# Index scores summed straight from PSUM, with the u projection moved behind them, in a hybrid decoder layer

## The chip, the cores and the metric

The kernel runs on one core of a Trainium2 chip. The metric is device time in microseconds (us) of one execution. TensorE is PE in the profile, ScalarE is ACT, VectorE is DVE, GpSimd is POOL, SyncE is SP, which issues the DMAs. SBUF is the on-chip memory; PSUM takes the results of matmuls, in 8 banks of 512 fp32 columns on each of 128 partitions.

## The reference, cut to what matters

One decoder layer over 1024 tokens of width 1024. A projection of the normalised input gives u (512 columns, for a state-space head group "S5"), q, k and v (attention) and q_idx, k_idx, w_idx (8 index heads of 64). The index heads choose 256 keys for each query; attention (a softmax over those keys alone) and the complex state-space recurrence of S5 follow, then an output projection and a squared-ReLU MLP.

```python
def block(start):                       # 128 queries
    causal = key_pos[None, :] <= q_pos[:, None]
    logits = jax.nn.relu(jnp.einsum('bthd,bsd->bths', qib, k_idx_f))
    score = jnp.einsum('bth,bths->bts', wb, logits) * IDX_SCALE
    score = jnp.where(causal[None], score, -jnp.inf)
    _, sel = lax.top_k(score, topk)     # topk = 256
    ...

h = rms_norm(x, norm1_g[i]) * (1.0 + sc1) + sh1
u_ssm, q, k, v, q_idx, k_idx, w_idx = jnp.split(h @ w_in[i], split_points, axis=-1)
y_ssm = s5_mixer(u_ssm, lam_re[i], lam_im[i], log_dt[i], ssm_b_re[i], ssm_b_im[i],
                 ssm_c_re[i], ssm_c_im[i], d_skip[i], w_glu[i], b_glu[i])
y_att = dsa_attention(q, k, v, q_idx, k_idx, w_idx, q_gain[i], k_gain[i])
mixed = jnp.concatenate([rms_norm(y_ssm, gn_ssm[i]), rms_norm(y_att, gn_attn[i])], axis=-1)
x = x + g1 * (mixed @ w_out[i])
...
```

## The kernel before, in words

Every matmul of the projections is made of three (`mm3`, L90 to L92): the operands are split into a high part (`wh`, `hh`) and a low part (`wl`, `hl`) in fp32r. `load_w` fetches a weight in pieces `raw` (two buffers); ACT makes `wh`, POOL makes `wl` (six buffers each; a half of u or q needs four of each). The product has 128 tokens and 256 columns.

The stage of the change:

- `index_proj` works through c = 0 to 3, two index heads at a time. `index_q` projects the index queries of c + 1; `index_score` makes the scores of c for the query tiles qt = 2 to 7 (the first two tiles need no selection): TensorE multiplies against the high and the low part of the index keys (L551, L552) into two PSUM banks (`bank2`, tag S, two such pairs; `bank`, tag g, gives four single banks), ACT takes Relu times |w| into an SBUF tile `r` (L556), and DVE adds sign(w) times r to the score tile `sc` in SBUF (L558 for the first head, L560). At the end six DVE operations (L517) put the causal mask on the last 128 columns of each tile.
- `tab` is a generator of tables for the state-space part, eight of them (b = 0 to 7): GpSimd operations (`cx`, `cl`, `mx`, `mt`, `tx`, `pt`) and stores to memory. It is woven into `index_proj`, one step at a time, and then into the projections.
- `proj_qu` projects u in two halves (each tile of 128 tokens copied by ACT to `us`, L576, and stored by SP) and then q in two halves (copied by ACT, L590; squared by POOL).
- `select` finds a threshold a tile so that 256 scores pass it: `bn_stats` of the tiles, a first guess v and its step gs, then nine rounds of counting, three tiles on DVE (L711, L721) and three on ACT (Sign with a running sum, L707, L717), a last step on DVE with the eight largest values (L734 to L741), and a flag: `bad` is summed over the partitions by a small matmul, copied, and read by the engines, which skip a slower search if it is 0. `need` is how many of the tied scores to keep. Then each tile's mask is made: Sign on ACT (L785), a scan and three passes on DVE, a product on POOL (L790).
- Attention and the state-space part follow; attention's first matmuls transpose q (L1222), ACT copies them (`qT`, L1224).

The kernel is written as Python generators, interleaved by `weave`; a scheduler of the framework then puts the instructions of each engine in one fixed order when the program is built, by the priority at which each was written. Each engine, and SP's queue of DMA issues, works through its order from the front, and an instruction that waits holds those behind it. `issue_after` names an instruction after which the framework places others.

## Time and profile before

| | |
|---|---|
| median of 3 runs | 1361.43 us (1357.9 to 1364.48) |
| the profiled execution | 1360.31 us, its span 1358.5 us |
| busy share of the span | PE 90%, DVE 75%, ACT 45%, POOL 27% |
| granted clock of TensorE, mean | 0.942 of 2.4 GHz |
| index scores end | 241.9 us after the span's start |
| first copy of attention | 319.33 us |

A row of the trace names the line, the engine, the operation, the tile written and the tiles read, the shape, and then busy time and mean or start and duration. "[8.99 <-DMA raw<-w_in]" means that the engine stood idle for 8.99 us before it and that this DMA was what it waited for. PEclk is the share of full clock granted to TensorE.

### The profile page before, as it was taken

How to read it: one execution, taken by the hardware profiler on the slowest of the kernel's cores; microseconds unless marked ns; L12 is line 12 of the kernel's file. 1: busy time of each engine (PE TensorE's matmuls, PEld its weight loads, DVE VectorE, ACT ScalarE, POOL GpSimd, SP SyncE). 2: the span in 40 equal slices, each digit the busy share in tenths (PEclk: the TensorE clock that was granted, in tenths of full speed). 3: DMA queues.
4: the chain of work that ended last, by engine and by line, in shares of the span. 5: the costliest groups of instructions: out<-in, count | busy, mean ns of one | idle time of the engine just before them, and what ended most of it. 6: DMA issues, size and time to landing. Idle time of an engine off the chain costs nothing.

```text
span 1358.5 us, 18554 instructions
## 1 busy us (share of the span) xinstructions
PE 1216.1 (90%) x6414; PEld 1038.1 (76%) x6414; DVE 1017.4 (75%) x1894; ACT 616.7 (45%) x1231; POOL 364.7 (27%) x350
## 2 busy tenths in 40 slices
PE   4987987935898999999979999999988999999997
PEld 4876887934788889888857788888866878788785
DVE  6599947897978763347795677677678888876887
ACT  6454453584777775724242333333224334333330
POOL 3072799861643453711100000000000000000125
PEclk9797989975899997999989999999998999999999
DMA  9511122350231572422412444433457735436252
GB/s 330 131 41 40 60 97 91 133 149 9 71 103 51 179 231 71 133 78 93 160 66 93 148 146 163 155 141 138 163 197 275 254 95 193 132 95 210 84 185 109
DMA packets 119327, 179.83 MB, mean 132 GB/s; under 512 B 28864, under 2 KB 63680, under 8 KB 119232
## 3 DMA queue, kind: packets, MB, share of 16 engines
q1 hardware_dynamic: 118160, 178.61, 40.1%
q8 instruction: 50, 0.82, 0.3%
q14 instruction: 45, 0.37, 0.1%
q10 hardware_dynamic: 1072, 0.03, 0.0%
HBM read 128.92 MB, written 48.50 MB: 131 GB/s over the span
## 4 chain that ended last, share of the span: by engine, by line
PE 51%; DVE 12%; DMA 4%; ACT 2%; issue 2%; POOL 2%; SPq 1%; DVEq 0%; ACTq 0%; POOLq 0%
PE pS L90 10%; PE pS L91 10%; PE pS L92 10%; PE pg L90 5%; PE pg L91 5%; PE pg L92 5%; DMA awa<-w_ada 2%; PE po L1274 2%; DVE fm L472 2%; PE pg L269 1%; PE pg L1258 1%; DVE acc L1871 1%; DVE acc L1845 1%; DVE fw L472 1%; POOL wol L472 1%
## 5 line engine op out<-in xcount | busy, mean ns | idle before, releaser
L1845 POOL TENSOR_TENSOR acc<-acc,g 128x512 f32<-128x512 f32 x4 | 5.9, 1499 | 579.1 <-DVE acc L1871 579.1
L91 PE MATMUL pg<-wl,hh 128*128 128x256 f32 (+1 forms) x288 | 81.6, 284 | 13.0 <-POOL wl L472 13.0
L470 ACT ACTIVATE fm<-ar 128x512 fp32r<-128x512 f32 x56 | 34.9, 624 | 119.9 <-PE pg L91 55.1
L90 PE MATMUL pg<-wh,hh 128*128 128x256 f32 (+1 forms) x288 | 81.0, 285 | 3.7 <-ACT wh L470 2.6
L1274 PEld LDWEIGHTS po<-v,pt 128*128 128x128 f32 x576 | 77.5, 208 | 6.0 <-ACT pt L1261 3.8
L1274 PE MATMUL po<-v,pt 128*128 128x64 f32 x576 | 78.8, 285 | 3.5 <-ACT pt L1261 3.3
L92 PE MATMUL pg<-wh,hl 128*128 128x256 f32 (+1 forms) x288 | 81.4, 284 | 0.0
L560 DVE SCALAR_TENSOR_TENSOR sc<-r,wsgn,sc 128x384 f32<-128x384 f32 (+5 forms) x42 | 56.0, 1344 | 28.5 <-ACT r L556 27.3
L90 PE MATMUL pS<-fm 128*128 128x512 f32 x160 | 62.2, 400 | 4.7 <-DVE z L1874 4.4
L91 PEld LDWEIGHTS pg<-wl,hh 128*128 128x128 f32 x288 | 55.1, 191 | 14.0 <-POOL wl L472 13.4
L91 PE MATMUL pS<-fm 128*128 128x512 f32 x160 | 63.1, 397 | 0.3 <-DVE fm L472 0.3
L92 PE MATMUL pS<-fm 128*128 128x512 f32 x160 | 62.9, 395 | 0.0
L1245 DVE CUSTOM_DVE_ANT_0 P<-pS,sc,rq 128x384 f32<-128x384 f32 (+5 forms) x48 | 43.9, 941 | 20.9 <-PE pS L1241 12.8
L90 PEld LDWEIGHTS pg<-wh,hh 128*128 128x128 f32 x288 | 54.3, 190 | 5.0 <-ACT wh L470 2.8
L556 ACT ACTIVATE r<-pS,wabs 128x384 f32<-128x384 f32 (+5 forms) x48 | 40.6, 848 | 36.4 <-PE pS L552 27.7
L92 PEld LDWEIGHTS pg<-wh,hl 128*128 128x128 f32 x288 | 54.9, 191 | 0.4
L470 ACT ACTIVATE fw<-ax 128x512 fp32r<-128x512 f32 x42 | 26.2, 623 | 61.1 <-PE pS L91 29.6
L1261 ACT ACTIVATE pt<-pg 128x512 f32<-128x512 f32 (+1 forms) x80 | 42.2, 547 | 22.2 <-PE pg L1258 21.8
L1258 PE MATMUL pg<-ident,P 128*128 128x128 f32 x288 | 49.2, 292 | 3.0 <-DVE zl L1340 1.3
L1247 ACT ACTIVATE P<-P,mx 128x128 f32<-128x128 f32 (+7 forms) x64 | 49.1, 769 | 5.7 <-DVE mx L1245 5.5
L90 PE MATMUL pS<-woh,mh 128*128 128x512 f32 x128 | 51.2, 400 | 0.0
L92 PE MATMUL pS<-woh,ml 128*128 128x512 f32 x128 | 50.9, 398 | 0.0
(606 smaller groups left out, 4154.1 us busy)
## 6 DMA issues: line engine op xcount, KB each, us to landing
awa<-w_ada SPq DMA_DIRECT2D x32, 512.0 KB, 4.3
a_d<-ws SPq DMA_DIRECT2D x64, 256.0 KB, 2.7
wr<-w_ff SPq DMA_DIRECT2D x32, 512.0 KB, 6.3
w1r<-w_ff SPq DMA_DIRECT2D x15, 1024.0 KB, 5.2
ax<-a_d SPq DMA_DIRECT2D x56, 256.0 KB, 2.8
ar<-a_d SPq DMA_DIRECT2D x56, 256.0 KB, 2.9
a_d<-c SPq DMA_DIRECT2D x45, 256.0 KB, 2.0
x<-x SPq DMA_DIRECT2D x16, 512.0 KB, 5.1
```

The lines of the kernel that those rows point to most:

```text
L90: T.matmul(out, lh, rh, start=start, stop=False, **kw)
L91: T.matmul(out, lh, rl, start=False, stop=False, **kw)
L92: self.pe = T.matmul(out, ll, rh, start=False, stop=stop, **kw).ins
L470: nc.scalar.activation(hi, x, AF.Copy)
L472: e.tensor_tensor(lo, x, f(hi), op=OP.subtract)
L556: S.activation(rv, ps[:, :, :n], AF.Relu, scale=self.wabs[:, qt, h:h + 1])
L560: V.scalar_tensor_tensor(sc, rv, self.wsgn[:, qt, h:h + 1], sc, op0=OP.mult, op1=OP.add)
L1245: V.tensor_tensor_reduce(pv, ps[:, :nj, :m], bv, scale=self.rq[:, qt, h:h + 1], scalar=-NEG, op0=OP.add, op1=OP.min, accum_out=mx)
L1247: S.activation(p[:, :w], p[:, :w], AF.Exp, scale=-1.0, bias=mx, accum_out=LS[qt][:, h:h + 1])
L1258: T.transpose(ps[:, o:o + 128], P[n][h][:, (k0 + i) * 128:(k0 + i + 1) * 128], self.ident)
L1261: S.activation(pt[:, :m], ps[:, :m], AF.Copy)
L1274: T.matmul(po[:, o:o + HD], pt[:, (2 * i + h) * 128:(2 * i + h + 1) * 128], self.v[:, k0 + i, kv * HD:(kv + 1) * HD], start=(o == 0 and k0 ...
```

## The change

1. `index_score` works on one bank at a time: tiles of up to 512 keys take a single bank from tag g, the others a pair whose halves are handled apart. Relu is written in place in PSUM; DVE reads it there and adds into `sc`. The tile `r` is gone. For h = 0 the last 128 columns get the mask as an addend (0 or NEG) in the same operation, and the six mask operations at the end go. ACT has 80 Relus in place of 48, DVE 86 operations in place of 54.
2. The matmuls of u are placed behind the last score matmul (`issue_after`).
3. Only four tables are woven into `index_proj`. From b = 4 on each begins with a small GpSimd copy from `self.gate`, which is `gs` for b = 4, 5, 6 and `need` for b = 7, and no table step is taken in the projections before the gate is set.
4. The rounds of `select` update t and v one column at a time.
5. The flag's matmul and copy become a DMA of `bad` (128 floats) into one row and a DVE maximum.

```diff
-LATER, TABN = 500, 1
+LATER, TABN, TABG = 500, 1, 4
...
-            self.index_proj(ix, tab)
+            self.gate = None
+            self.index_proj(ix, itertools.islice(tab, 10 * TABG))
...
-                next(tab, None)
+                if self.gate is not None and i < 29:
+                    next(tab, None)
...
-        nc.vector.tensor_scalar(self.caus, io, 0.0, 0.5, op0=OP.is_le, op1=OP.subtract)
-        nc.vector.tensor_scalar(self.caus, self.caus, -NEG, 2.0, op0=OP.mult, op1=OP.mult)
+        nc.vector.tensor_scalar(self.caus, io, 0.0, NEG, op0=OP.is_gt, op1=OP.mult)
...
-        for qt in range(2, 8):
-            dg = self.bias[qt][:, qt * 128:]
-            V.scalar_tensor_tensor(dg, dg, NEG, self.caus, op0=OP.max, op1=OP.min)
...
         nc = self.nc
         V, S, G, T = nc.vector, nc.scalar, nc.gpsimd, nc.tensor
         for qt in range(2, 8):
-            n = (qt + 1) * 64
+            w = (qt + 1) * 128
+            nj = 1 if w <= 512 else 2
+            n = w // nj
             for i in range(2):
                 h = 2 * c + i
-                ps = self.bank2()
+                ps = self.bank()[:, None, :] if nj == 1 else self.bank2()
                 lq = qs[c][i][:, (qt - 2) * 128:(qt - 1) * 128]
-                for j in range(2):
+                for j in range(nj):
                     o = ps[:, j, :n]
-                    T.matmul(o, lq, self.kih[:, j * n:(j + 1) * n], start=True, stop=False)
-                    T.matmul(o, lq, self.kil[:, j * n:(j + 1) * n], start=False, stop=True)
-                sc = self.bias[qt].rearrange("p (j n) -> p j n", j=2)
-                r = ix.tile([128, L], F32, name="r", tag="r", bufs=3)
-                rv = r[:, :2 * n].rearrange("p (j n) -> p j n", j=2)
-                S.activation(rv, ps[:, :, :n], AF.Relu, scale=self.wabs[:, qt, h:h + 1])
-                if h == 0:
-                    V.tensor_scalar(sc, rv, self.wsgn[:, qt, h:h + 1], None, op0=OP.mult)
-                else:
-                    V.scalar_tensor_tensor(sc, rv, self.wsgn[:, qt, h:h + 1], sc, op0=OP.mult, op1=OP.add)
+                    ks = slice(j * n, (j + 1) * n)
+                    T.matmul(o, lq, self.kih[:, ks], start=True, stop=False)
+                    self.last_sc = T.matmul(o, lq, self.kil[:, ks], start=False, stop=True).ins
+                    S.activation(o, o, AF.Relu, scale=self.wabs[:, qt, h:h + 1])
+                    sc, sg = self.bias[qt][:, ks], self.wsgn[:, qt, h:h + 1]
+                    if h:
+                        V.scalar_tensor_tensor(sc, o, sg, sc, op0=OP.mult, op1=OP.add)
+                        continue
+                    d = n - 128 if j == nj - 1 else n
+                    V.tensor_scalar(sc[:, :d], o[:, :d], sg, None, op0=OP.mult)
+                    if d < n:
+                        V.scalar_tensor_tensor(sc[:, d:], o[:, d:], sg, self.caus, op0=OP.mult, op1=OP.add)
                 yield
 
     def proj_qu(self):
...
-                for k in range(KC):
-                    wh, wl = wg[k]
-                    self.mm3(ps[:, :256], self.hh[:, k, tl], self.hl[:, k, tl], wh, wl, k == 0, k == KC - 1)
+                with self.tc.issue_after(self.last_sc):
+                    for k in range(KC):
+                        wh, wl = wg[k]
+                        self.mm3(ps[:, :256], self.hh[:, k, tl], self.hl[:, k, tl], wh, wl, k == 0, k == KC - 1)
...
+        self.gate = gs
...
-        ps = self.bank()
-        T.matmul(ps[0:1, 0:1], bad, self.ones[:, 0:1], start=True, stop=True)
+        row = sp.tile([1, 128], F32, name="row")
+        nc.sync.dma_start(row, bad)
-        V.tensor_copy(fi, ps[0:1, 0:1])
+        V.tensor_reduce(fi, row, axis=AX.X, op=OP.max)
...
+        self.gate = need
...
+            if b >= TABG:
+                G.tensor_copy(cx[:, 0, 0:6], self.gate)
```

TensorE before, in the scores of c = 1: score matmuls (pS) and, between them, matmuls of the u projection (pg, with wh and wl of w_in).

```order
L92 MATMUL pg_2199<-wh_2183,hl_125 128x256
L90 MATMUL pg_2199<-wh_2189,hh_124 128x256
L551 MATMUL pS_1708<-kih_135,qs_1427 128x256
L552 MATMUL pS_1708<-kil_136,qs_1427 128x256
L551 MATMUL pS_1708<-kih_135,qs_1427 128x256
L552 MATMUL pS_1708<-kil_136,qs_1427 128x256
L91 MATMUL pg_2199<-wl_2190,hh_124 128x256
```

TensorE after the change, in the scores of c = 2 and 3 (single banks are named pg here too), and where the scores end:

```order
L553 MATMUL pS_1906<-kih_134,qs_1652 128x320
L554 MATMUL pS_1906<-kil_135,qs_1652 128x320
L553 MATMUL pg_2023<-kih_134,qs_1843 128x384
L554 MATMUL pg_2023<-kil_135,qs_1843 128x384
L553 MATMUL pS_1922<-kih_134,qs_1653 128x320
L554 MATMUL pS_1922<-kil_135,qs_1653 128x320
L553 MATMUL pg_2029<-kih_134,qs_1844 128x384
L554 MATMUL pg_2029<-kil_135,qs_1844 128x384
L553 MATMUL pg_2034<-kih_134,qs_1843 128x512
```

```order
L553 MATMUL pS_2107<-kih_134,qs_1844 128x512
L554 MATMUL pS_2107<-kil_135,qs_1844 128x512
L91 MATMUL pg_2156<-wh_2134,hh_123 128x256
L92 MATMUL pg_2156<-wl_2135,hh_123 128x256
L93 MATMUL pg_2156<-wh_2134,hl_124 128x256
```

No u matmul stands between scores any more; the first (wh, hh) comes right behind the last score matmul.

POOL before, where u's second half has its last two low parts (wl_2538, wl_2544); cx, cl, mt, tx and pt belong to tables:

```order
L1025 TENSOR_TENSOR cx_1931<-A2_619,Li_949 128x576 [waits Pool_49]
L472 TENSOR_TENSOR wl_2538<-raw_2535,wh_2537 128x512 [waits Activation_49]
L472 TENSOR_TENSOR wl_2544<-raw_2541,wh_2543 128x512 [waits DMAHW7_49,Activation_49]
L1056 TENSOR_TENSOR pt_1863<-e1c_950,e2c_952 128x256 [waits DMAHW4_49]
L1056 TENSOR_TENSOR pt_1863<-e1c_950,e2s_953 128x256
L1027 TENSOR_TENSOR cl_1930<-A1_618,Lr_948 128x576 [waits DMAHW5_49]
L1059 TENSOR_TENSOR pt_1863<-pt_1863,tx_1864 128x256 [waits Pool_49] x2
```

POOL after the change, where u's second half has its last two low parts (wl_2496, wl_2502); gs is the selection's, and the tables are 4 and 5. First the gate, then the weights:

```order
L1053 TENSOR_TENSOR mt_1958<-mt_1958,mx_1959 128x512 [waits Pool_49]
L1066 TENSOR_TENSOR pt_2000<-pt_2000,tx_2001 128x256 [waits Pool_49] x2
L1034 TENSOR_TENSOR cl_2350<-A1_617,Lr_947 128x576 [waits DMAHW1_49,Pool_49]
L1051 TENSOR_TENSOR mt_2459<-D1_555,Lr_947 128x512 [waits DMAHW2_49,Pool_49]
L1029 COPY cx_2351<-gs_2314 128x6 [waits DVE_49]
L1049 TENSOR_TENSOR mx_2460<-D2_556,Li_948 128x512
```

```order
L1063 TENSOR_TENSOR pt_3034<-e1c_949,e2c_951 128x256 [waits DMAHW3_49]
L1063 TENSOR_TENSOR pt_3034<-e1c_949,e2s_952 128x256
L1053 TENSOR_TENSOR mt_2905<-mt_2905,mx_2906 128x512 [waits Pool_49]
L1066 TENSOR_TENSOR pt_3034<-pt_3034,tx_3035 128x256 [waits Pool_49]
L474 TENSOR_TENSOR wl_2496<-raw_2493,wh_2495 128x512 [waits Activation_49]
L1066 TENSOR_TENSOR pt_3034<-pt_3034,tx_3035 128x256 [waits Pool_49]
L474 TENSOR_TENSOR wl_2502<-raw_2499,wh_2501 128x512 [waits Activation_49]
```

Before, the low parts of u's second half stood between operations of tables that wait for no gate; now the gate of tables 4 and 5 stands ahead of them.

ACT after the change, in the last of the selection's rounds (ja with c is a count, t and v its update); wh_ are high parts of q's first half, us tiles of u:

```order
L580 ACTIVATE us_2716<-pg_2691 128x256 [waits DMAHW1_49,PE_49]
L724 ACTIVATE v_2308<-t_2310,v_2308,st2_2317 128x1 [waits Activation_49]
L723 ACTIVATE t_2310<-c_2309,oA_1260 128x1 [waits Activation_49]
L722 ACTIVATE ja_2213,c_2309<-sc4_103,v_2308 128x640
L724 ACTIVATE v_2308<-t_2310,v_2308,st2_2317 128x1 [waits Activation_49]
L723 ACTIVATE t_2310<-c_2309,oA_1260 128x1 [waits Activation_49]
L722 ACTIVATE ja_2213,c_2309<-sc6_105,v_2308 128x896
L580 ACTIVATE us_2763<-pg_2738 128x256 [waits DMAHW3_49,PE_49]
L724 ACTIVATE v_2308<-t_2310,v_2308,st2_2317 128x1 [waits Activation_49]
L472 ACTIVATE wh_2833<-raw_2831 128x512 [waits DMAHW5_49,PE_49,Pool_49]
```

The high parts stand between counts of the selection, and each waits for TensorE (PE) to give a buffer back.

## Rows read from the trace of the kernel before

**Rows 1.** The page, busy us (share of span) xinstructions of each engine.

```profile
PE 1216.1 (90%) x6414; PEld 1038.1 (76%) x6414; DVE 1017.4 (75%) x1894; ACT 616.7 (45%) x1231; POOL 364.7 (27%) x350
```

**Rows 2.** Windows: stretch, us, busy (instructions) PE, PEld, DVE, ACT, POOL, PEclk, DMA share, GB/s.

```profile
160.00:200.00 40.00, 34.11 (x250) 33.20 (x250) 23.62 (x21) 19.35 (x31) 40.00 (x34) 0.91 0.23 78
200.00:240.00 40.00, 32.88 (x241) 31.65 (x240) 28.18 (x20) 17.87 (x27) 40.00 (x31) 0.91 0.31 102
280.00:300.00 20.00, 5.91 (x51) 5.71 (x49) 19.88 (x68) 19.97 (x60) 13.91 (x23) 0.75 0.58 160
300.00:320.00 20.00, 1.99 (x11) 1.99 (x12) 18.50 (x78) 0.69 (x2) 0.65 (x4) 0.50 0.24 71
320.00:340.00 20.00, 16.19 (x97) 14.62 (x96) 13.53 (x49) 14.18 (x45) 5.33 (x8) 0.64 0.04 8
340.00:360.00 20.00, 16.79 (x134) 15.27 (x132) 19.06 (x45) 17.80 (x41) 13.16 (x11) 1.00 0.22 53
```

**Rows 3.** Timeline of ACT and DVE: start us, us, instruction, idle before and releaser.

```profile
197.67 0.63 ACT L470 ACTIVATE wh<-raw 128x512 fp32r<-128x512 f32 x1 [8.99 <-DMA raw<-w_in]
...
240.39 1.51 DVE L560 SCALAR_TENSOR_TENSOR sc<-r,wsgn,sc 128x1024 f32<-128x1024 f32 x1 [9.59 <-ACT r L556]
```

**Rows 4.** The page, costliest groups: count, busy us, mean ns, idle before, releaser.

```profile
L91 PE MATMUL pg<-wl,hh 128*128 128x256 f32 (+1 forms) x288 | 81.6, 284 | 13.0 <-POOL wl L472 13.0
...
L560 DVE SCALAR_TENSOR_TENSOR sc<-r,wsgn,sc 128x384 f32<-128x384 f32 (+5 forms) x42 | 56.0, 1344 | 28.5 <-ACT r L556 27.3
```

**Rows 5.** Groups by shape, 113 to 243 us, DVE and ACT, columns as in rows 4.

```profile
L517 DVE SCALAR_TENSOR_TENSOR sc<-sc,caus 128x128 f32<-128x128 f32 x6 | 5.0, 827 | 0.2
L538 DVE TENSOR_TENSOR qs<-pg,qs 64x512 fp32r<-64x512 f32 x7 | 4.8, 686 | 0.1
L538 DVE TENSOR_TENSOR qs<-pg,qs 64x256 fp32r<-64x256 f32 x8 | 3.4, 422 | 0.3
...
L558 DVE TENSOR_SCALAR sc<-r,wsgn 128x1024 f32<-128x1024 f32 x1 | 0.7, 749 | 0.0
...
L556 ACT ACTIVATE r<-pS,wabs 128x1024 f32<-128x1024 f32 x8 | 8.9, 1115 | 4.4 <-PE pS L552 4.4
...
L556 ACT ACTIVATE r<-pS,wabs 128x384 f32<-128x384 f32 x8 | 4.6, 581 | 4.3 <-PE pS L552 4.2
```

**Rows 6.** Lines 576 and 590, the copies of u and q: durations min/median/max ns, first and last start.

```profile
L576 ACT ACTIVATE us<-pg x16: 369/383/388, 153.9 to 226.9; 128x256 f32<-128x256 f32 x16
...
L590 ACT ACTIVATE q<-pg x16: 361/383/391, 242.8 to 286.1; 128x256 f32<-128x256 f32 x16
```

**Rows 7.** Timeline of PE in the q projection, two matmuls with 24 between them.

```profile
279.77 0.28 PE L90 MATMUL pg<-wh,hh 128*128 128x256 f32 x1
...
282.70 0.28 PE L91 MATMUL pg<-wl,hh 128*128 128x256 f32 x1
```

**Rows 8.** Timeline of ACT: the selection's first and last round, attention's first copy, first mask.

```profile
257.37 1.04 ACT L707 ACTIVATE ja<-sc,v 128x896 bf16<-128x896 f32 x1 [6.57 <-DVE v L698]
...
299.70 0.39 ACT L719 ACTIVATE v<-t,v,st 128x1 f32<-128x1 f32 x1
...
319.33 0.60 ACT L1224 ACTIVATE qT<-pg 128x512 fp32r<-128x512 f32 x1 [19.24 <-PE pg L1222]
322.71 0.61 ACT L785 ACTIVATE ja<-sc,ntau 128x384 bf16<-128x384 f32 x1 [2.79 <-DVE ntau L779]
```

**Rows 9.** Line 1029, one operation of each of the eight tables, columns as in rows 6.

```profile
L1029 POOL TENSOR_TENSOR cl<-cl,cx x8: 1398/1792/2275, 155.4 to 273.5; 128x576 f32<-128x576 f32 x8
```

**Rows 10.** Groups of lines 787 to 789 on DVE, 320 to 372 us, columns as in rows 4.

```profile
L787 DVE TENSOR_TENSOR_SCAN pre<-eq 128x384 f16<-128x384 bf16 (+5 forms) x6 | 9.7, 1615 | 0.1
...
L788 DVE TENSOR_SCALAR eq<-pre,need 128x384 bf16<-128x384 f16 (+5 forms) x6 | 3.3, 552 | 0.0
L789 DVE TENSOR_TENSOR eq<-eq,ja 128x384 bf16<-128x384 bf16 (+5 forms) x6 | 3.2, 538 | 0.0
```

**Rows 11.** DMA issues: queue, operation, count, KB each, median us from issue to landing.

```profile
dg<-d_skip SPq DMA_DIRECT2D x8, 4.0 KB, 2.6
```

**Rows 12.** Windows, one stretch ahead of the scores, columns as in rows 2.

```profile
92.00:96.00 4.00, 2.42 (x12) 1.69 (x11) 3.86 (x10) 1.42 (x9) 2.02 (x3) 1.00 0.52 132
```

More of the change, by code (lines that the diff above doesn't have):

```diff
@@ L1 @@
+import itertools
 from contextlib import ExitStack
@@ L440, in k_norm @@
         self.rstd(rk, self.kss[:, 4 * hf:4 * hf + 4].rearrange("p t h -> p (t h)"), HD, ix)
-        knd = ix.tile([128, NKV, 4, 2, HD], F32, name="knd", tag="r", bufs=3)
+        knd = ix.tile([128, NKV, 4, 2, HD], F32, name="knd", bufs=2)
         yield
@@ L694, in select @@
         V.tensor_tensor(sd, va, y, op=OP.mult)
-        v, d, c, t = st(6, "v"), st(NV, "d"), st(6, "c"), st(6, "t")
+        v, c, t = st(6, "v"), st(6, "c"), st(6, "t")
         V.tensor_tensor(v, sd, self.zrow, op=OP.mult)
@@ L711, in select @@
             V.tensor_scalar(jv[:, :W[i]], B[i], col(v, i), None, op0=OP.is_ge, op1=OP.add, accum_out=col(c, i))
-        V.scalar_tensor_tensor(t[:, :NV], c[:, :NV], TOPK - 0.5, gs[:, :NV], op0=OP.subtract, op1=OP.mult)
-        V.tensor_tensor(v[:, :NV], v[:, :NV], t[:, :NV], op=OP.add)
+            V.tensor_scalar(col(t, i), col(c, i), TOPK - 0.5, col(gs, i), op0=OP.subtract, op1=OP.mult)
+            V.tensor_scalar(col(v, i), col(v, i), col(t, i), None, op0=OP.add)
         yield
@@ L721, in select @@
                 V.tensor_scalar(jv[:, :W[i]], B[i], col(v, i), None, op0=OP.is_ge, op1=OP.add, accum_out=col(c, i))
-            V.tensor_tensor(d, v[:, :NV], st1[:, k, :NV], op=OP.subtract)
-            V.scalar_tensor_tensor(t[:, :NV], c[:, :NV], float(TOPK), st2[:, k, :NV], op0=OP.is_ge, op1=OP.mult)
-            V.tensor_tensor(v[:, :NV], d, t[:, :NV], op=OP.add)
+                V.tensor_scalar(col(t, i), col(c, i), float(TOPK), st2[:, k, i:i + 1], op0=OP.is_ge, op1=OP.mult)
+                V.tensor_scalar(col(v, i), col(v, i), st1[:, k, i:i + 1], col(t, i), op0=OP.subtract, op1=OP.add)
             yield
```

## The prediction

> **What bounds the kernel now.** I read the busy shares first [rows 1]. TensorE leads with 90%, yet a share over the whole span says nothing about one stage, so I went to the stretches of the stage that the change touches [rows 2]. From 160 to 240 us TensorE is busy for 34.1 and 32.9 of each 40 us while DVE has only 23.6 and 28.2, and GpSimd is full. There TensorE does index scores and the u projection in turn, and both wait for GpSimd: ACT stands idle for 8.99 us until a raw piece of w_in lands, DVE for 9.59 us before its very last score [rows 3]; over the kernel TensorE loses 13.0 us to wl<-raw on GpSimd [rows 4]. The last score ends at 240.39 + 1.51 = 241.9 us [rows 3]. Then the picture turns over: from 280 to 320 TensorE works 5.9 and 2.0 us of 20 and its clock is at 0.50, half of 2.4 GHz, while DVE is full. The q projection is over (its last copy starts at 286.1 [rows 6]) and attention cannot start, because the flag's matmul stands ahead of it in TensorE's order: ACT takes the first qT only at 319.33, after 19.24 us of idling, and the first mask at 322.71 [rows 8]. So the stage is a chain: scores until 241.9, selection until about 318, attention after it, with TensorE empty for some 30 us.
>
> **Scores, c = 1 to 3.** The adds that read r and sc from SBUF average 1344 ns [rows 4]. They now read PSUM and one SBUF tile. The nearest rows are the subtractions qs<-pg, one PSUM and one SBUF input, made in the same stretch beside the same full GpSimd: 422 ns for 256 columns, 686 for 512 [rows 5], that is 0.16 us + 1.03 ns a column. A head's ten pieces (384, 512, and twice 320, 384, 448 and 512) cost 5.9 us against 6 x 1.344 = 8.1; six heads save 12.7 us. DVE's 23.6 + 28.2 = 51.8 us after 160 [rows 2] become 39.1. ACT gets four more Relus a head: 1115 and 581 ns for 1024 and 384 columns [rows 5] leave 0.26 us fixed, so six heads add 6.3 us; the u copies that leave (16 x 0.383 [rows 6]) take about as much out; ACT stays near 37 us. TensorE, rid of u, is no longer the bound: 16,896 columns a c at 0.457 ns (25 matmuls of 256 columns in 2.93 us [rows 7]) are 7.7 us. With GpSimd's weights out of the way the last score then ends at 160 + 39 = 199 us; a pair of PSUM banks is now held until DVE has read it, so I take **200** (194 to 212).
>
> **c = 0 and the mask: nothing.** The h = 0 products read PSUM instead of SBUF. From SBUF 1024 columns took 749 ns [rows 5], so 4,224 columns cost 3.1 us at least; by the PSUM price above they cost 5.9, with six more pieces 1.0 on top. The Trainium skill, VectorE: DVE Perf Modes, section "Why PSUM operands drop a tier", speaks against the change here: a PSUM operand holds an fp32 operation to one element a cycle. By the SBUF price this part would gain 3 us, by that rule it costs about what I have. Against the 3.8 us lost stand the six mask operations, 5.0 us [rows 5], which are gone.
>
> **Projections.** Held behind the last score matmul, u and q now run in one piece. Sixteen q copies from 242.8 to 286.1 [rows 6] are 2.89 us each, 23.1 a half; four halves 92.4 us from 199 on. The cost is the price of what hid u before: all 46 us of it lay under the scores. Then the gate. GpSimd waits for gs. The way from the last add to the first Sign takes 257.4 - 241.9 = 15.5 us now [rows 3, 8]; as the other tiles' statistics are placed among the last scores I take 8 (4 to 15). Behind gs stand tables 4 and 5 and behind these the weights wl of u's second half. Eight tables take 155.4 to 273.5, 16.9 us apiece with a wl in each [rows 9]; at the fastest row's pace, 1398 against a median of 1792, some 13. Two, less what stands ahead of the gate, are 21 to 28 us, so wl comes at 231 to 238, while TensorE wants it at 199 + 23.1 + 1.4 = 223.5: a hole of 7 to 14, I take **11** (none if gs is early and DVE quiet, 25 if gs is late). Projections end at 199 + 92 + 11 = **302**.
>
> **Selection.** From first Sign to last v 299.7 - 257.4 = 42.3 us, then 23.0 to the first mask [rows 8]. ACT's order now has the wh pieces of q between the Signs, and these wait until TensorE frees a buffer at the end of u's second half, about 200 + 55; the last round follows, so the first mask stands at about 200 + 81 = 281. The masks' scans, compares and products take DVE 9.7 + 3.3 + 3.2 us [rows 10]; all lies before 302. So the DMA in the flag's place costs nothing: at 2.6 us for a small load (dg<-d_skip [rows 11]; a matmul and a copy before) the projections hide it, and were selection last it would cost 2 to 4 us. The per-column operations lie beside ACT's longer chain: nothing. The gate on need holds the last table to about 276, and SP's loads for the state-space part stand behind its three stores, but attention comes first: nothing, or the store's few us if they are late.
>
> **What follows.** Attention starts at 302 instead of 318.7 (the first qT's wait ended): 17 us. Its first 40 us were slow: TensorE had 16.2 of 20 at a clock of 0.64, then 16.8 of 20 [rows 2]. A TensorE that never stopped enters at full clock: 16.2 x 0.36 = 5.8 us at most; the masks no longer share DVE, which is full at 340 to 360: at most the 7 us that TensorE idles. I take 8 of these (0 to 13). **Sum: 25 us.** Against the profiled 1360.3 that is 1335; the median of the runs is 1.1 higher, so **1336**.
>
> **The rivals.**
> - *Bank turns (slower).* Relu in place holds each pair of banks through TensorE, ACT and DVE: 4 x 0.23, then 2 x 0.69, then 0.69 for the last half [rows 5, 7], 3.0 us, of which half is gained if the two pairs overlap fully. If only one is ever in flight, eight pairs are 24 us a c and 26 with the singles: scores end at 160 + 78 = 238, projections at 340, and 21 - 8 = 13 us are lost: **1374**. It decides from a last score at 225 on, where nothing is left. For it: u no longer fills TensorE's waits. Against: ACT sits between and both halves have their own operations. 0.15.
> - *The gate starves TensorE (same).* The 13.0 us of wl [rows 4] show how easily GpSimd's order holds TensorE. A hole of 25 instead of 11, and 5 more at q's weights, end the projections at 321; the warm clock is all that is left: gain 0 to 8, **1357**. 0.17.
> - *A cold clock in the scores.* TensorE had 2.42 of 4 us busy at clock 1.00 once [rows 12] and 2.0 of 20 at 0.50 [rows 2]; the scores would give it 7.7 of 13. At half clock a c is 15.4 us, more than DVE's 11.9: 10.5 us later, **1347**. The Trainium skill, TensorE: Matmul & The Clock Gate, section "A second HAM failure mode: psum-queue depth-cycling", describes this: short idling between groups that turn through PSUM lets the clock fall again and again. Rows at a like share are all at 1.00. 0.08.
> - *More is freed.* No hole, the last score at 194, and all 13 us of the attention's start: 38 to 45 us, **1320**. 0.10.
> - That the hold isn't in the order is excluded: no score stands behind the first u matmul.
>
> **How the numbers follow.** The forecast has 0.50 and by itself 1322 to 1352. Half a per cent is 6.8 us, about what a measurement of this kernel can tell from none. Faster: 0.50 + 0.08 + 0.10 and a quarter of the gate's 0.17, 0.72; same 0.13; slower 0.15. The range 1314 to 1362 leaves out the bank rival and the far end of the last one.
>
> **What would show it.** Last score by 194 to 212, and scores' adds near 0.5 to 0.7 us; TensorE without scores after it and one hole of 7 to 14 us before wl of u's second half; a first qT at about 302 with the clock at 1.00. I am wrong if the last score ends after 225, if the copies of q end after 315, or if attention starts near 302 and the end still does not move.

## The result: 1 per cent slower, with the scores ending 16 us earlier

The changed kernel takes 1374.1 us (median of 5 runs, 1372.6 to 1377.3) against 1358.8 of before on the same chip: 1.0103 of the time, 95% interval 1.0079 to 1.0128, some 14 us slower where 25 us less was forecast. Its profiled execution has a span of 1371.6 us (1358.5 before).

The busy shares on the page of the changed kernel, columns as in [rows 1]:

```profile
PE 1246.1 (91%) x6380; PEld 1045.2 (76%) x6380; DVE 1015.7 (74%) x1953; ACT 621.2 (45%) x1263; POOL 341.7 (25%) x354
```

TensorE has 30 us more of modelled busy time than before, with 34 instructions less, and the kernel is slower: the share tells nothing of a gain, for a matmul at a lower clock counts as busy for longer (0.49 us a score matmul at 200 to 220 us, clock 0.50, against 0.30 at 0.91 in e5_warm). The stage has to be read by windows.

Windows of the changed kernel, columns as in [rows 2]:

```profile
160.00:200.00 40.00, 31.87 (x96) 20.09 (x94) 27.30 (x50) 23.87 (x45) 30.84 (x35) 0.76 0.17 56
200.00:220.00 20.00, 16.21 (x33) 8.32 (x34) 13.33 (x24) 9.85 (x17) 9.49 (x12) 0.50 0.14 51
240.00:260.00 20.00, 20.00 (x173) 20.00 (x172) 20.00 (x73) 18.23 (x52) 19.66 (x22) 1.00 0.53 169
260.00:280.00 20.00, 20.00 (x173) 20.00 (x172) 11.97 (x33) 18.11 (x52) 15.77 (x15) 1.00 0.54 165
280.00:300.00 20.00, 20.00 (x173) 20.00 (x172) 15.01 (x42) 5.07 (x14) 9.08 (x12) 1.00 0.17 55
300.00:320.00 20.00, 16.38 (x141) 16.14 (x139) 16.04 (x30) 4.22 (x10) 16.30 (x20) 1.00 0.19 63
320.00:340.00 20.00, 10.73 (x45) 8.86 (x46) 19.41 (x53) 12.30 (x36) 11.95 (x12) 0.62 0.17 47
```

From 160 to 200 us TensorE counts 31.9 us busy, nearly as before [rows 2], but with 96 matmuls instead of 250: u's are gone. From 200 to 220 it needs 16.2 busy us for 33 score matmuls, at a clock of 0.50, while DVE has 13.3 and ACT 9.9 of 20. No engine is full there. From 240 to 300 TensorE is full and the clock at 1.00.

The copies of u, of q, attention's first copies (line or tile views of the changed kernel, columns as in [rows 6]; the last row is the kernel before):

```profile
L580 ACT ACTIVATE us<-pg x16: 360/368/385, 228.1 to 271.9; 128x256 f32<-128x256 f32 x16
```

```profile
L594 ACT ACTIVATE q<-pg x16: 362/368/386, 278.9 to 323.1; 128x256 f32<-128x256 f32 x16
```

```profile
L1231 ACT ACTIVATE qT<-pg x16: 574/592/600, 323.9 to 515.8; 128x512 fp32r<-128x512 f32 x16
```

```profile
L1124 DVE COPY ug<-pg x8: 657/681/692, 348.3 to 426.2; 128x512 f32<-128x512 f32 x8
```

```profile
L1117 DVE COPY ug<-pg x8: 658/681/692, 336.7 to 414.6; 128x512 f32<-128x512 f32 x8
```

The last add starts at 225.4 and ends at 226.1, not near 200. The copies of u and q then run from 228 to 323. Attention's first qT stands at 323.9, 4.6 us later than before [rows 8], and the state-space part's first copy (ug) at 348.3 against 336.7: 11.6 us. The rest of the way adds one to two more, up to the span's 13.1.

The projections themselves end earlier than the copies tell. Around their end, TensorE and then ACT (timeline of the changed kernel; ja is the Sign of the fourth mask):

```profile
315.22 0.28 PE L93 MATMUL pg<-wh,hl 128*128 128x256 f32 x1
...
324.57 0.48 PE L1247 MATMUL pS<-kTh,qT 128*128 128x128 f32 x1 [8.20 <-ACT qT L1231]
```

```profile
321.94 0.94 ACT L790 ACTIVATE ja<-sc,ntau 128x768 bf16<-128x768 f32 x1 [6.81 <-DVE rw L622]
322.79 0.64 ACT L594 ACTIVATE q<-pg 128x256 f32<-128x256 f32 x2
323.93 0.59 ACT L1231 ACTIVATE qT<-pg 128x512 fp32r<-128x512 f32 x1
```

TensorE's last projection matmul starts at 315.2. The last two copies of q and the first qT stand in ACT's order behind a Sign that waits 6.8 us for DVE, and TensorE waits 8.2 us for qT.

What the scores wait for, changed kernel, 160 to 226 us (us in total, times, longest):

```profile
PEld pS L553 <- DVE sc L558: 31.8, 42, 1.9
ACT pS L555 <- PE pS L554: 24.7, 38, 1.8
DVE sc L558 <- ACT pS L555: 19.3, 34, 4.6
```

A ring, in which each engine waits for the next: TensorE waits for DVE's add, ACT for TensorE, DVE for ACT, each for 19 to 32 of 66 us. The timeline of the changed kernel shows one turn of it (tile of 640 keys, heads 6 and 7, halves of 320):

```profile
206.83 0.64 PE L553 MATMUL pS<-kih,qs 128*128 128x320 f32 x1
206.83 0.50 ACT L555 ACTIVATE pS<-pS,wabs 128x320 f32<-128x320 f32 x1 [0.84 <-PE pS L554]
...
207.37 0.55 DVE L558 SCALAR_TENSOR_TENSOR sc<-pS,wsgn,sc 128x320 f32<-128x320 f32 x1 [0.59 <-ACT pS L555]
...
207.97 0.64 PE L553 MATMUL pS<-kih,qs 128*128 128x320 f32 x1 [0.24 <-DVE sc L558]
...
209.45 0.55 DVE L558 SCALAR_TENSOR_TENSOR sc<-pS,wsgn,sc 128x320 f32<-128x320 f32 x1 [0.59 <-ACT pS L555]
...
210.05 0.69 PE L553 MATMUL pS<-kih,qs 128*128 128x384 f32 x1 [0.24 <-DVE sc L558]
```

At 207.97 TensorE starts the second half of head 6. It had waited for the add of the first half of head 6, which ended at 207.37 + 0.55 = 207.92. Nothing in the arithmetic asks for that: the two halves lie in different banks.

The order of the built programs says where the wait comes from. TensorE's rows of the changed kernel, c = 3, 640 keys, with what each waits for:

```
L553 MATMUL pS_2044<-kih_134,qs_1843 128x320 [waits DVE_49]
L553 MATMUL pS_2053<-kih_134,qs_1844 128x320 [waits DVE_49]
L553 MATMUL pS_2044<-kih_134,qs_1843 128x320 [waits DVE_49]
L553 MATMUL pS_2053<-kih_134,qs_1844 128x320 [waits DVE_49]
```

pS_2044 is one tile of two banks. The change writes, for each half, matmul, Relu, add, and then the next half's matmul: a write into a tile that ACT and DVE have just used, so the second half waits for the first half's add. (The kernel before wrote both halves before anything read them.) Of each pair one half is on its way at a time. I call this the link. (The "bank theory" below is that Relu in place holds the banks too long, the "depth theory" that two pairs are too few in any order.)

### The profile page after: what moved, and what is told of

It is laid out like the page before. It is cut to its first block, busy times and chain, and to the rows that moved or that the text cites. A ratio compares the mean times of both kernels' runs of the same rounds, so it can differ in the third digit from the quotient of the medians.

```text
span 1371.6 us, 18627 instructions
## 1 busy us (share of the span) xinstructions
PE 1246.1 (91%) x6380; PEld 1045.2 (76%) x6380; DVE 1015.7 (74%) x1953; ACT 621.2 (45%) x1263; POOL 341.7 (25%) x354
## 4 chain that ended last, share of the span: by engine, by line
PE 52%; DVE 10%; DMA 3%; issue 2%; ACT 2%; POOL 1%; SPq 0%; ACTq 0%; DVEq 0%; POOLq 0%
PE pS L91 10%; PE pS L92 10%; PE pS L93 10%; PE pg L91 5%; PE pg L92 5%; PE pg L93 5%; PE po L1281 3%; DVE fm L474 2%; PE pg L1265 1%; DMA awa<-w_ada 1%; PE pg L271 1%; DVE acc L1878 1%; DVE acc L1852 1%; PE pS L1247 1%; DMA ar<-a_d 1%
## 5 line engine op out<-in xcount | busy, mean ns | idle before, releaser
L553 PE MATMUL pS<-kih,qs 128*128 128x320 f32 (+3 forms) x64 | 36.6, 572 | 29.4 <-DVE sc L558 20.2
L553 PEld LDWEIGHTS pS<-kih,qs 128*128 128x128 f32 x64 | 16.0, 250 | 51.9 <-DVE sc L558 41.2
L555 ACT ACTIVATE pS<-pS,wabs 128x320 f32<-128x320 f32 (+3 forms) x64 | 36.9, 581 | 38.5 <-PE pS L554 37.8
L1247 PE MATMUL pS<-kTh,qT 128*128 128x384 f32 (+5 forms) x96 | 39.9, 418 | 13.7 <-ACT qT L1231 8.2
```

The costliest lines, as they stand in the source:

```text
L553: T.matmul(o, lq, self.kih[:, ks], start=True, stop=False)
L555: S.activation(o, o, AF.Relu, scale=self.wabs[:, qt, h:h + 1])
L1247: T.matmul(ps[:, j, :m], QT[qt][:, h, :], self.kTh[kv][:, sl], start=True, stop=False)
```

## The experiments

Times are set against the kernel before on the same chip, 1359 to 1362 us; two ratios that differ by 0.005 are at the edge of what these runs tell apart. The runs that gave a result, with the points of their traces (in before and e3_old_scores a mask operation follows the last add, 1.5 and 1.8 us later):

| run | last add starts | first qT | first ug | time, us | ratio to before (95%) |
|---|---|---|---|---|---|
| before | 240.4 | 319.3 | 336.7 | 1359 to 1362 | |
| the change | 225.4 | 323.9 | 348.3 | 1374.1 | 1.0103 (1.0079 to 1.0128) |
| e1_no_hold | 253.0 | 351.7 | 369.8 | 1388.3 | 1.0188 (1.0141 to 1.0235) |
| e3_old_scores | 214.7 | 315.8 | 335.8 | 1363.1 | 1.0002 (0.9978 to 1.0026) |
| e5_warm | 225.1 | 327.1 | 348.1 | 1368.2 | 1.0048 (1.0028 to 1.0068) |
| e2_no_gate | 224.0 | 332.5 | 350.9 | 1379.8 | 1.0131 (1.0085 to 1.0177) |
| g1_mm_first | 210.9 | 309.9 | 333.4 | 1361.5 | 1.0003 (0.9978 to 1.0028) |
| g2_pairs | 200.7 | 304.1 | 328.5 | 1344.1 | 0.9867 (0.9828 to 0.9905) |
| g4_allg | 203.5 | 302.6 | 327.1 | 1349.1 | 0.9922 (0.9890 to 0.9954) |
| g5_six | 198.1 | 297.6 | 321.5 | 1341.8 | 0.9868 (0.9825 to 0.9912) |
| g6_six_pairs | 202.1 | 299.9 | 325.6 | 1347.1 | 0.9899 (0.9870 to 0.9928) |
| f1_scores_alone | 251.4 | 319.8 | 340.6 | 1367.4 | 1.0049 (1.0021 to 1.0077) |
| f2_six_alone | 199.7 | 300.2 | 322.4 | 1348.0 | 0.9913 (0.9882 to 0.9944) |
| h1_ja2 | 197.3 | 296.8 | 318.8 | 1347.2 | 0.9914 (0.9886 to 0.9943) |
| h2_six_no_hold | 198.4 | 296.4 | 317.1 | 1342.2 | 0.9866 (0.9834 to 0.9898) |
| h3_six_no_gate | 199.0 | 301.9 | 322.5 | 1352.1 | 0.9943 (0.9923 to 0.9964) |
| h4_six_flag | 199.4 | 314.2 | 333.1 | 1352.3 | 0.9922 (0.9895 to 0.9950) |

From the first ug to the end the profiled executions take 1016 to 1027 us (1022 before), in no order that follows the edits. A few us of a time can come from there, and no run was made on it.

### What holds the scores: the clock, or the banks

**e5_warm** lifts the clock by more work: each score's first product is made twice and the first one thrown away.

```diff
+                    T.matmul(o, lq, self.kih[:, ks], start=True, stop=True)
                     T.matmul(o, lq, self.kih[:, ks], start=True, stop=False)
```

> The change with each score's first matmul made twice (the first product is thrown away), which only adds work to TensorE, half as many matmuls again. Clock theory: more activity lifts the granted clock in the scores towards 1.00, and the last score comes 5 to 20 us earlier than 225 with more work done: 1355 to 1370. Bank theory: each turn of a bank is longer by the extra matmul, the last score comes at 230 to 245: 1378 to 1395.

Windows and waits of this run, columns as above:

```profile
180.00:200.00 20.00, 15.17 (x60) 9.60 (x60) 15.51 (x28) 12.65 (x24) 20.00 (x24) 1.00 0.22 83
200.00:220.00 20.00, 15.34 (x52) 9.11 (x52) 13.37 (x24) 10.30 (x18) 6.94 (x8) 0.91 0.07 27
```

```profile
PEld pS L553 <- DVE sc L559: 27.7, 40, 1.5
```

One turn of 640 keys, from a half's matmul to the next half's:

```profile
206.28 0.41 PE L553 MATMUL pS<-kih,qs 128*128 128x320 f32 x1 [0.41 <-DVE sc L559]
...
208.16 0.42 PE L553 MATMUL pS<-kih,qs 128*128 128x320 f32 x1
```

The clock is 1.00 and 0.91 where the change had 0.71 (180 to 200) and 0.50, and the ring is still there. The last add starts at 225.1: nothing gained, nothing lost. This does not measure the clock by itself, for the third matmul takes TensorE's time back (15.3 us busy at 200 to 220, 16.2 in the change); the turn is 1.88 us here and 2.08 in the change (207.97 to 210.05). It does show that the ring stands at a high clock too. That the clock fell because TensorE kept waiting in the ring fits this and g5_six below, whose scores run at 1.00 without the ring. Neither theory had its time: the run is 7 us faster than the change, though the first ug comes at the same time in both (348.1 and 348.3); why was not followed.

**e3_old_scores** takes the scores' code of before (the lines with - of the diff in `index_score`, `caus` and the six mask operations), all else as changed.

```diff
...
-                    S.activation(o, o, AF.Relu, scale=self.wabs[:, qt, h:h + 1])
...
+                S.activation(rv, ps[:, :, :n], AF.Relu, scale=self.wabs[:, qt, h:h + 1])
...
```

> The change with the scores of before (Relu into an SBUF tile, DVE adds from SBUF, mask operations at the end), hold, gates and flag as changed. Bank theory: banks come free at Relu, the last score comes at about 205 and the time falls to 1345 to 1360. Clock theory: TensorE still works in short pieces, the clock is still at 0.50 to 0.8 and the last score at 220 or later: 1370 to 1385, as DVE's adds are slower on top.

```profile
160.00:180.00 20.00, 14.59 (x54) 11.42 (x54) 19.45 (x17) 12.35 (x17) 20.00 (x16) 0.72 0.07 28
180.00:200.00 20.00, 13.72 (x51) 9.91 (x50) 19.48 (x15) 10.22 (x13) 20.00 (x14) 0.74 0.15 55
```

The slow form, DVE's adds from SBUF, starts its last add at 214.7, 11 us before the form that was to be faster, at a clock no better than the change's (0.72 and 0.74). It is bound by what the sum said: DVE has 19.5 of 20 us. So the loss sits in the PSUM form. The last add came some 10 us later than the bank theory had it, and the time at before's. The run is also the hold, the gates and the flag without the PSUM scores: the last add starts 26 us earlier than before, but qT only 3.5 and ug 0.9 us earlier, and the time is the same. Scores that end earlier are not yet time gained.

**g1_mm_first** keeps each operation of the change and alters their order in a pair:

```diff
                 for j in range(nj):
                     T.matmul(o, lq, self.kih[:, ks], start=True, stop=False)
                     self.last_sc = T.matmul(o, lq, self.kil[:, ks], start=False, stop=True).ins
-                    S.activation(o, o, AF.Relu, scale=self.wabs[:, qt, h:h + 1])
-                    ...
+                for j in range(nj):
+                    S.activation(o, o, AF.Relu, scale=self.wabs[:, qt, h:h + 1])
+                for j in range(nj):
+                    ...
```

> The change with the same operations in another order within a pair of banks: the matmuls of both halves first, then both Relus, then both adds. Link theory (the pair is one tile, so as the change writes it the second half's matmul waits for the first half's add, and only one half of each pair is ever on its way): that wait is gone, TensorE waits once a pair and both pairs are in flight; the last score comes at 200 to 212 instead of 225, and the time falls by 8 to 20 us to 1354 to 1366. Depth theory (two pairs are too few as long as Relu stays in PSUM, whatever the order): the last score stays at 218 or later and the time within 4 us of the change.

TensorE's rows of the built program, c = 3, 768 keys: only the first half waits.

```
L553 MATMUL pS_2062<-kih_134,qs_1843 128x384 [waits DVE_49]
L553 MATMUL pS_2062<-kih_134,qs_1843 128x384
L553 MATMUL pS_2071<-kih_134,qs_1844 128x384 [waits DVE_49]
L553 MATMUL pS_2071<-kih_134,qs_1844 128x384
```

The last add moves from 225.4 to 210.9, the time by 0.0100 of before's (about 14 us) to that of before. The link is shown, by an edit of the written order alone. Its share by itself is smaller and clearest at the end: the last 40 of the 160 score matmuls take 19.5 us (188.7 to 208.2) instead of 23.6 (200.4 to 224.0), at a clock about as low (0.65 from 190 to 200 and 0.50 from 200 to 210). Some 8 of the 14 us are gained in the first 40, where DVE is full (9.7 of 10 us from 120 to 130) with other work as well, which the scheduler orders anew; and from 150 to 160 the clock is 1.00 instead of 0.54, so wait and clock are not parted there. And the waits of g1_mm_first in 160 to 215 us still read

```profile
PEld pS L553 <- DVE sc L563: 24.3, 17, 7.2
ACT pS L557 <- PE pS L554: 21.4, 14, 7.6
```

and the last add is at 211, not 200: with two Relus and two adds a pair, two pairs turn too slowly even when both are in flight. Four more runs are on that.

**g4_allg** gives every half a single bank of its own, order as changed; **g5_six** puts the matmuls first and the two heads of a c into different banks:

```diff
+                if nj == 2 and i:
+                    pt = self.bank2()
+                    ob = [pt[:, j, :n] for j in range(nj)]
+                else:
+                    ob = [self.bank()[:, :n] for j in range(nj)]
...
```

> The change with every half in a single bank of its own (tag g, four of them), the pairs unused in this stage, order of the operations as changed. Link theory: no half shares a tile with another, four are in flight: last score at 200 to 212, 1354 to 1366. Depth theory: four banks are as many as two pairs: 218 or later, 1370 or more.

> Matmuls first, and the two heads of a c in different banks: the first in two single banks, the second in a pair, eight banks in all. Link theory: little beyond the run with the matmuls first, ACT and DVE are the bound: last score at 197 to 208, 1348 to 1362. Depth theory: this alone moves the score's end, to 205, and 1350 to 1362, while the runs with four banks stay near the change. If the end of the scores moves by 15 us or more and the time by less than 5, what bounds is behind them: masks on DVE, or the projections.

**g2_pairs** has the two pairs of g1_mm_first with one Relu and, for all heads but the first, one add over both halves:

```diff
+                pv = ps[:, :, :n]
+                S.activation(pv, pv, AF.Relu, scale=self.wabs[:, qt, h:h + 1])
...
+                    V.scalar_tensor_tensor(sc, pv, sg, sc, op0=OP.mult, op1=OP.add)
...
```

> As the run with the matmuls first, but one Relu and (for all heads but the first) one add over both halves of a pair. Link theory: no second half waits either; fewer operations (0.26 us fixed on ACT, 0.16 on DVE saved a pair), but Relu waits for both halves: last score at 200 to 215, 1352 to 1368. Depth theory: 220 or later, 1372 or more.

**g6_six_pairs** is g5_six with that for the second head.

> The run with eight banks, the second head's pairs with one Relu and one add over both halves. DVE is busy for 19.97 of 20 us at 180 to 200 there, so fixed costs count: 12 pairs of c = 1 to 3 save 12 x 0.16 us on DVE and 12 x 0.26 on ACT, the last score 1 to 3 us earlier, 1337 to 1342. If the longer Relu holds up the turn instead: last score at 194 or later, 1342 to 1348.

g5_six (four single banks and two pairs, all eight), windows and the copies of q:

```profile
160.00:180.00 20.00, 18.77 (x92) 14.36 (x92) 15.55 (x27) 15.32 (x30) 20.00 (x23) 1.00 0.29 97
180.00:200.00 20.00, 16.57 (x90) 12.48 (x91) 19.97 (x41) 13.23 (x25) 20.00 (x24) 1.00 0.25 88
```

```profile
L603 ACT ACTIVATE q<-pg x16: 362/373/388, 247.5 to 293.0; 128x256 f32<-128x256 f32 x16
```

Now DVE is the bound of the scores (19.97 of 20 us beside a full POOL) at a clock of 1.00, the last add starts at 198.1, q ends at 293, and the kernel takes 1341.8 us, 18 us less than before. g4_allg has four banks like g1_mm_first and is 11 us faster: the depth theory in its strict form falls, since single banks come free one by one. g2_pairs, too, does better than g1_mm_first, by 17 us, with the same two pairs of banks and Relu in place: its last add starts at 200.7. So more banks are one cure and fewer, wider operations a turn another; which part of a turn g2_pairs saves was not followed. g4_allg, g5_six and g2_pairs all took less time than any theory had given them. In g6_six_pairs the last add came 4 us later than g5_six's, the second of its two expectations: there the longer Relu and add cost more than their fixed costs save.

**f1_scores_alone** puts the scores as changed, **f2_six_alone** those of g5_six, into the kernel before, without hold, gates or new flag.

> The kernel before with the scores exactly as the change writes them (halves linked), u ungated and unheld, eight tables, old flag. Link theory: the link alone makes the change slower; last score later than the 241.9 of before by 5 to 20 us and 1368 to 1395 (the change without its hold gave 1388). If the loss came from the hold or the gates instead: 1355 to 1362 or faster, as the mended scores alone gave 1348.

> The kernel before with one part of the change, PSUM scores in the mended form (matmuls first, the two heads in different banks, mask as an addend); u still among the scores, eight ungated tables, the old flag. If the scores' form alone makes the gain: last score by 215 and 1340 to 1348. If TensorE and the weights behind GpSimd's tables hold the scores there whatever DVE does (13.0 us of waits for wl before): last score at 228 to 242 and 1350 to 1362; then the gain needs the hold and the gate as well.

The linked scores alone end at 251.4, 11 us later than before's, and the kernel is slower by 0.5%; the end is in the link theory's range, the time (1367) just under it. The mended ones alone end at 199.7 and take 12 us off; hold, gates and flag together add 6 us to that in g5_six, at the edge of what the intervals part. POOL's order, which I took for a bound of the scores in the kernel before, does not hold them here, with POOL at 20.0 of 20 us from 160 to 200 as before.

### The other parts: hold, gates, flag, masks

**e1_no_hold** and **h2_six_no_hold** take the hold away, from the change and from g5_six.

```diff
-                with self.tc.issue_after(self.last_sc):
-                    for k in range(KC):
+                for k in range(KC):
...
```

> The change without its hold: u's matmuls may stand between the scores again, all else as changed. Clock theory (with u gone TensorE works in short pieces, its clock falls to 0.50 and the scores run at half speed): the granted clock from 176 to 224 us goes from 0.50-0.84 back to 0.9 or more, the last score comes at 225 or earlier although u lies among the scores, q alone stands behind it and ends near 275 instead of 323, and the time is 1330 to 1350. Bank theory (in-place Relu holds the PSUM banks, whatever the clock): the last score comes later than 225, by 10 us or more, and the time is 1350 to 1365. Mask theory (the loss is made at 320 to 348, by the gated table and the masks): 1365 to 1374, with attention starting as late as now.

> The run with eight banks, without the hold. If the hold is what brings selection forward (u's 46 us of TensorE delay the scores one for one when they stand between them): last score at 215 to 235, TensorE idle before attention again, 1350 to 1365. If u would fit into the scores' gaps once the banks turn freely: last score by 205, projections at 275 to 285, 1330 to 1341.

With linked scores the hold is worth some 12 us: without it u goes between the scores, the last add starts at 253.0, selection ends later, and TensorE stands still for 61 us before attention (its first matmul with qT is the last line):

```profile
220.00:240.00 20.00, 20.00 (x164) 19.94 (x163) 8.16 (x16) 8.03 (x17) 1.97 (x2) 1.00 0.22 67
```

```profile
352.33 0.47 PE L1246 MATMUL pS<-kTh,qT 128*128 128x128 f32 x1 [60.79 <-ACT qT L1230]
```

The time was outside all three ranges: I had counted on u being done early, but attention waits for selection, not for u. With the banks mended the hold is worth nothing (1342.2 against 1341.8). The last add starts at 198.4 without it, but this run hardly puts u among the scores: its first u matmul starts at 191.4 (194.7 with the hold). What keeps u back until then was not followed.

**e2_no_gate** and **h3_six_no_gate** weave all eight tables as before.

```diff
-LATER, TABN, TABG = 500, 1, 4
+LATER, TABN, TABG = 500, 1, 8
...
-                if self.gate is not None and i < 29:
-                    next(tab, None)
+                next(tab, None)
```

> The change without the gates: all eight tables are woven as before, hold and PSUM scores as changed. Mask theory (the last table behind need, and the masks behind it, delay attention's and the state-space part's start by some 7 us): 1362 to 1368. Clock and bank theories: the scores end as late as now or later, since GpSimd is full and index weights wait for it: 1372 to 1385.

> The run with eight banks, without the gates. The linked form lost 5 us without them, as the weights of u waited for tables. If that holds here too: u's second half and q late by 5 to 8 us, 1345 to 1352. If the gate's own waits cost as much (need holds the last table until 277): 1336 to 1343.

What POOL waits for, longest first: e2_no_gate, 226 to 332 us, then the change, 226 to 325:

```profile
POOL wl L473 <- ACT wh L471: 19.9, 7, 9.5
POOL qsq L595 <- ACT q L593: 15.8, 7, 7.8
```

```profile
POOL cx L1029 <- DVE gs L704: 18.0, 1, 18.0
```

Without gates both kernels are slower, by 4 us (within the intervals) and by 10. In h3_six_no_gate the first ug comes only 1.0 us later than in g5_six, so most of its 10 us lie behind that point and are not explained. In the change POOL waits 18.0 us for gs, and TensorE has no wait for POOL in that stretch: the gate costs nothing there.

**h4_six_flag** puts the flag's matmul back into g5_six.

```diff
-        row = sp.tile([1, 128], F32, name="row")
-        nc.sync.dma_start(row, bad)
+        ps = self.bank()
+        T.matmul(ps[0:1, 0:1], bad, self.ones[:, 0:1], start=True, stop=True)
...
```

> The run with eight banks, with the flag's matmul and copy in place of the DMA. TensorE takes the flag's matmul in its order behind the projections (end near 293) while bad is ready at 270.7: if it is placed behind them, the masks begin 15 to 20 us later and the time is 1350 to 1362; if the scheduler places it among the projections, near its own time, or the masks were not what attention waits for: 1338 to 1346.

The flag is ready at 272.0, and the masks start at 292.3, behind the projections; attention's qT comes at 314.2. The trace loses 12 us at the first ug against g5_six; the ratios differ by 0.005, the edge of what they tell.

**h1_ja2** gives the masks' Sign tile a second buffer.

```diff
-            sn = sp.tile([128, L], BF, name="ja", tag="ja")
+            sn = sp.tile([128, L], BF, name="ja", tag="ja", bufs=2)
...
```

> The run with eight banks, plus a second buffer for the tile into which ACT writes a mask's Sign. Mask theory (attention's first qT copy stands on ACT behind a Sign that waits for DVE to leave the one buffer, and TensorE idles 11 us for it): that wait is gone, qT comes 3 to 6 us earlier than 297.6, and the time falls by 2 to 8 us to 1334 to 1340. If DVE's own order holds attention anyway: qT earlier, but the time within 3 us of 1342.

ACT in g5_six, where attention's first qT stands behind a Sign that waited for DVE (timeline, columns as in [rows 3]):

```profile
296.71 0.94 ACT L799 ACTIVATE ja<-sc,ntau 128x768 bf16<-128x768 f32 x1 [3.36 <-DVE eq L803]
297.56 1.06 ACT L1240 ACTIVATE qT<-pg 128x512 fp32r<-128x512 f32 x2
```

The second buffer moved qT by 0.8 us only and took no time off (1347 against 1342, not told apart): the Signs still wait for DVE. TensorE waits 11.0 us for the first qT in both runs; in f2_six_alone, where the first mask comes behind the first qT (304.1 and 300.2), it waits 0.4. No run moves the masks behind qT and changes nothing else. Attention's start stays slow: from the first qT to the first ug it takes 23.9 us in g5_six, 24.4 in the change, 17.4 before. Which of the interleaved works there (masks, the last reciprocal roots for q, attention) sets it is open.

## Why the prediction was wrong

- **Last score at 200: the step that failed.** The sum took DVE's work as the time, and gave the bank turns 1 us on top ("I take 200"). The price of the adds was nearly right (forecast 0.69 and 0.49 us for 512 and 320 columns beside a full POOL, measured 0.75 and 0.55, below), but no engine set the pace: the ring did, and the scores ended at 226. With the link cut they end at 212 (g1_mm_first), with the link cut and more banks at 199 (g5_six), which is the forecast's number, with DVE full as the sum had it.

```profile
L558 DVE SCALAR_TENSOR_TENSOR sc<-pS,wsgn,sc 128x512 f32<-128x512 f32 x14 | 10.5, 750 | 5.3 <-ACT pS L555 5.2
...
L558 DVE SCALAR_TENSOR_TENSOR sc<-pS,wsgn,sc 128x320 f32<-128x320 f32 x14 | 7.6, 546 | 2.6 <-ACT pS L555 2.5
```

- **The bank rival** named the right cause, the turns of the banks, and its point of decision held ("from a last score at 225 on", nothing is left). That its time is the measured one, 1374, is luck: it had one pair in flight, every pair of a c at the price of the widest, scores to 238 and projections to 340, and then 8 us gained at attention's start. Measured are two halves in flight, one of each pair, scores to 226, the first qT 4.6 us late, and 7 us lost at attention's start. I gave it 0.15 because "both halves have their own operations". They had; what I did not ask is what a half's matmul waits for. The rows with their waits, which name DVE at every half, were there to be read before the run.
- **Cold clock.** It came (0.71 at 180 to 200, 0.50 at 200 to 220 us), where I had priced it at 10 us and held it unlikely because "rows at a like share are all at 1.00". They are not: in the kernel before TensorE has 2.55 of 4 us busy at 0.50 from 320 to 324. What it cost here by itself is open; e5_warm shows that with a third matmul in each turn and the clock at 0.91 to 1.00 the scores end no earlier, and g1_mm_first that the last 40 score matmuls take 4 us less of 24 at a clock about as low, once the link is cut. The Trainium skill, TensorE: Matmul & The Clock Gate, section "A second HAM failure mode: psum-queue depth-cycling", tells of a clock that falls in short idling between groups that turn through PSUM. The trace agrees as to the clock (0.50 at 200 to 220 us); how much of the scores' delay the clock made, no run here shows.
- **The hole of 11 us before u's second half** did not come: gs is there at 229.8, 4 us behind the last add instead of 8, the last two low parts of u's second half start at 250.1 and 252.1, 20 and 22 us behind gs, at the near end of the forecast's 21 to 28, and TensorE is full from 240 to 300. (The forecast's own terms, 199 + 8 and 21 to 28, give 228 to 235 for wl, 3 us less than it states.) TensorE had the four halves done at 315.5, 89 us behind the last add (226.1) against 92 + 11: the one error of the sum on the good side.
- **Selection and flag:** the first mask came as forecast, at 302.7, 77 us behind the last add (81 forecast). That the masks cost nothing, since "all lies before 302", failed: the six take from 302.7 to 345.0, each Sign waits for DVE, and the last copies of q and the first qT stand behind them on ACT. TensorE was done at 315.5, and attention's qT came at 323.9. The flag's DMA costs nothing, as forecast, but the old form had been priced too low: put back, its matmul stands behind the projections and costs attention 12 us in the trace.
- **The start of attention, 8 us gained: wrong by its sign.** The clock is 1.00 up to 320, but TensorE stands still for 8.2 us from 316 on; from 320 to 340 the clock is 0.62 and DVE has 19.4 us, where the masks still lie among attention's operations on ACT and DVE (the last product starts at 344.0). That the masks are what slows it is read from the order and not shown by a run. From first qT to first ug 7 us were lost.
- **The sum with the measured terms:** the last add ends at 226.1, the projections' matmuls 89 us later, the masks on ACT add 8: the first qT at 323.9 instead of 319.3, 4.6 us late; 7 us at attention's start; one to two behind it: 13.1 of the span.

## What to carry to other kernels

When an operation moves into a multi-bank PSUM tile, ask of each instruction in the built order what it waits for: a tile is guarded as a whole, and writing one part after another has been used joins the parts into one turn. Issue all matmuls of such a tile before anything reads it, or give each part its own tile. A stage in which no engine is full and each waits for the next is bound by the turn, the sum of its steps on all engines, and not by the busiest engine's work. A step made cheaper on one engine saves only its share of a turn; here more turns in flight (g5_six, g4_allg) or fewer operations a turn (g2_pairs) gave the time back. And an operation placed early, as the masks here, can stand ahead of what the next stage waits for: look at the order of the engine that both share.

## What was not expected of the hardware

Half as many matmuls again in the scores raised the granted clock from 0.50 to 0.91 (200 to 220 us) and moved the scores' end by 0.3 us: in this stage the low clock came with the waits of the ring, and lifting it in this way did not shorten it. And DVE's add of 512 columns from one PSUM and one SBUF operand took 0.74 us in g5_six beside a POOL that was busy for 20.0 of 20 us, where the same add from SBUF alone took 1.28 in e3_old_scores beside a POOL as busy and kept DVE full (means of 160 to 200 and of 160 to 216 us):

```profile
L567 DVE SCALAR_TENSOR_TENSOR sc<-pg,wsgn,sc 128x512 f32<-128x512 f32 x10 | 7.2, 744 | 0.4 <-ACT pg L561 0.4
```

```profile
L563 DVE SCALAR_TENSOR_TENSOR sc<-r,wsgn,sc 128x512 f32<-128x512 f32 x5 | 6.4, 1277 | 0.2
```
